# Moving the large tiles by 32 bytes, and four ways to run the products of the last feed-forward

## The chip, the cores and the metric

The kernel runs on one core of a Trainium2 chip. The metric is the device time of one execution in microseconds; the number of a kernel is the median of its runs.

## What is computed

The reference is one inference step of a small hybrid transformer (two layers, model width 2048) for 128 context tokens and 128 latent tokens. The even layer mixes by latent attention and grouped-query attention, the odd one by differential attention. Both end in the same gated feed-forward, the part that the change touches most:

```
def conv_ffn(h, w_up, w_conv, b_conv, w_down):
    u = h @ w_up
    up = jnp.pad(u, ((0, 0), (1, 1), (0, 0)))
    u = up[:, :-2] * w_conv[0] + up[:, 1:-1] * w_conv[1] + up[:, 2:] * w_conv[2] + b_conv
    gate, val = u[..., :D_FF], u[..., D_FF:]
    return (jax.nn.silu(gate) * val) @ w_down
...
    x = x + gt1 * m
    h = rmsnorm(x, g_norm_ffn[l]) * (1 + sc2) + sh2
    x = x + gt2 * conv_ffn(h, w_ffn_up[l], w_ffn_conv[l], b_ffn_conv[l], w_ffn_down[l])
```

All arrays are float32. D_FF is 5632, so w_up has 2048 x 11264 elements and w_down 5632 x 2048.

## The kernel before

Features lie on the 128 partitions and tokens along the row: the 128 context and 128 latent tokens together make 256 columns (NT). Each weight matrix comes in blocks of 128 x 128. One output chunk of 128 features is a product over KD = 16 blocks (up) or KQ = 22 blocks (down).

**Three matmuls per block.** Every float32 operand is split into a high part, rounded to the matmul's type float32r, and a low part, the rest. `split` (lines 243 to 245) does it: ScalarE casts, VectorE subtracts. Weights arrive by DMA in `raw` tiles of 1 MB and are split into `wh` and `wl`, four buffers each of 8 blocks. Activations are kept split, the high 256 columns and the low 256 columns side by side in one row of ROW = 512 elements: `hx` for the input of a stage, one tile `g` per 128 features for the input of the down product. `gemm` (line 330) then issues three matmuls per block into one accumulator bank `acc`: high weights by high columns, high weights by low columns, low weights by high columns. All matmuls pass through line 104, so the profile shows them under that line and they are told apart by their tiles: `acc<-hx,wh` and `acc<-hx,wl` in the up product, `acc<-g,wh` and `acc<-g,wl` in the down product. `acc` has three banks.

**The feed-forward** (`ffn`, line 1226) runs twice, l = 0 and l = 1. The hidden features are done in NQ = 2 halves. For each half, `up` makes 22 pairs of gate and value chunks (44 products of 48 matmuls), and `conv` (line 1236) takes each from its bank by one ScalarE and two VectorE operations; the gated result is split into a `g` tile. Then `down` makes 16 chunks (16 products of 66 matmuls), and `residual` (line 753) adds each to `x` by two VectorE operations, one per token group (L755 in the profile). In the last half of l = 1 ScalarE also squares each finished chunk for the final norm. The first three products of each up stage are made before `ffn` begins, beside the norm, and handed over in `ready`.

**The tail.** After the last chunk's residual come the square (L196), four small matmuls, the root (L208, L211), a diagonal (L231), a spread over the partitions by matmul, and the final scaling (L1348, L1346) with the output DMAs.

**The order.** The instructions of each engine are ordered by a scheduler that simulates the program's timeline, except where `keep_order` pins an instruction to the program's order. DMAs of weights are issued on the SP queue.

**Where tiles lie.** `cst`, the packed constants, is the first tile of the pool `keep`; all other tiles come behind it and start at multiples of 32 bytes. `cst` has 1397 columns, 5588 bytes, and the next tile `x` starts at byte 6752 of each partition. Two unused pads stand in the program: 48 columns ahead of the weight buffers, and SHIFT = 320 bytes ahead of `cv` and `g` (and of `hxc` and `u`). The `g` tiles have one name with 22 rotating buffers.

Of the kernel before, what the change touches and what calls it, by code (L numbers as in the profile page):

```python
# [11 lines left out]
F32R = mybir.dt.float32r  # L12
# [5 lines left out]
P = 128  # L18
# [3 lines left out]
NT = 2 * T  # L22
ROW = 2 * NT
SHIFT = 320
NL = 2
# [6 lines left out]
NQ = 2  # L32
KQ = NFF // NQ
# [6 lines left out]
    ("cond", 32), ("bada", NL * 6 * KD),  # L40
    ("gmix", NL * KD), ("gffn", NL * KD), ("gfin", 16),
    ("gmq", 6), ("gmkv", 4), ("gqn", 1), ("gkn", 1), ("lam", 4),
    ("gsub", 256),
]
_AT = {}
_n = 0
# [42 lines left out]
def step_kernel(ctx: ExitStack, tc: tile.TileContext, A: dict):  # L89
# [4 lines left out]
    def keep_order(i):  # L94
        if not any(i is j for j in kept):
            kept[:] = [i]
            tc.keep_in_program_order(i)
# [16 lines left out]
    pe = TensorE()  # L114
# [5 lines left out]
    pacc = ctx.enter_context(tc.tile_pool(name="pacc", bufs=3, space=PSUM))  # L120
# [5 lines left out]
    def banks(name):  # L126
        return tc.tile_pool(name=name, bufs=1, space=PSUM)
# [3 lines left out]
    def nm(s):  # L131
        uid[0] += 1
        return f"{s}_{uid[0]}"

    def T_(pl, shape, tag, dt=F32, bufs=None):
        kw = {} if bufs is None else {"bufs": bufs}
        return pl.tile(shape, dt, tag=tag, name=nm(tag), **kw)
# [18 lines left out]
    x = T_(keep, [P, KD, NT], "x")  # L156
# [31 lines left out]
    def stat_add(st, src, n, eng=pool):  # L188

        st["n"] += 1  # L190
        if st["n"] == 1:
            st["acc"] = T_(keep, [P, NT], "sqacc")
            act.activation(st["acc"], src, AF.Square)
            return
        sq = T_(tmp, [P, NT], "sq", bufs=2)
        act.activation(sq, src, AF.Square)  # L196
        if st["n"] == n:
            st["last"] = sq
        else:
            eng.tensor_tensor(out=st["acc"], in0=st["acc"], in1=sq, op=ALU.add)  # L200
# [126 lines left out]
            pin(pe.matmul(ps[c][:, :NT], wl, xh(k), start=False, stop=b))  # L327
        return [p[:, :NT] for p in ps]

    def gemm(blocks, xh, xl, n=NT, first=0, between=None):  # L330

        fixed = lambda i: keep_order(i) if between is not None else i
        ps = T_(pacc, [P, 512], "acc")
        last = len(blocks) - 1
        for i in range(last + 1):
            k = (i + first) % (last + 1)
            wh, wl = blocks[k]
            fixed(pe.matmul(ps[:, :n], wh, xh(k), start=(i == 0), stop=False))  # L340
            fixed(pe.matmul(ps[:, :n], wh, xl(k), start=False, stop=False))
            if callable(between):
                if i == (last + 1) // 2:
                    between()
            elif between and i in between:
                between[i]()
            fixed(pe.matmul(ps[:, :n], wl, xh(k), start=False, stop=(i == last)))
        return ps[:, :n]


# [209 lines left out]
    def pump(rows, feats=0.0, until=None):  # L560

        until = until or RLIMIT[stage[0]]
        step()
        side_pump()
        ada["due"] += rows
        while ada["due"] >= 0.25:
            if ada["i"] >= until and not later:
                ada["due"] = 0.0
                break
            ada["due"] -= 0.25 if ada["i"] >= until else 0.25 * ada["pew"]  # L570
            row_step(until)
        feat["due"] += feats
        while feat["due"] >= 1.0 and feat["i"] < FLIMIT[stage[0]]:
            feat["due"] -= 1.0
            feature_step()
# [176 lines left out]
    def residual(ps, l, which, c, st=None):  # L752
        for g in range(2):
            s = slice(g * T, (g + 1) * T)
            dve.scalar_tensor_tensor(out=x[:, c, s], in0=ps[:, s],  # L755
                                     scalar=mod[:, l, 3 * which + 2, c, g:g + 1],
                                     in1=x[:, c, s], op0=ALU.mult, op1=ALU.add)
        if st is not None:
            stat_add(st, x[:, c], KD)
# [465 lines left out]

    def ffn(hx, W, ready, turn, l, st):
        xh, xl = (lambda k: hx[:, k, :NT]), (lambda k: hx[:, k, NT:2 * NT])
        product = lambda: ready.pop(0) if ready else gemm(W.chunk(), xh, xl, between=in_order.pop(0) if in_order else None)
        WD = Weights(A["w_down"][l], KQ, TB)
        cw = ada["cw"]  # L1230
        with tc.tile_pool(name=f"ffn{l}", bufs=1) as fp, banks(f"pffn{l}") as pf:
            feat["home"], feat["pool"] = fp, pf
            feat["due"] = 0.0
            in_order = [{}, {}] + turn + [{}]
            T_(fp, [P, SHIFT // 4], "pad")

            def conv(m):
                early = bool(ready)
                pin = keep_order if early else lambda i: i
                ps = product()  # L1240
                y = T_(fp, [P, NT], "cv", bufs=3)
                pin(act.activation(y, ps, AF.Identity, scale=cw[:, 1, m:m + 1], bias=cw[:, 3, m:m + 1]))  # L1242
                y3 = y.rearrange("p (g t) -> p g t", g=2)
                p3 = ps.rearrange("p (g t) -> p g t", g=2)
                pin(dve.scalar_tensor_tensor(out=y3[:, :, 1:], in0=p3[:, :, :T - 1],  # L1245
                                             scalar=cw[:, 0, m:m + 1], in1=y3[:, :, 1:],
                                             op0=ALU.mult, op1=ALU.add))
                pin(dve.scalar_tensor_tensor(out=y3[:, :, :T - 1], in0=p3[:, :, 1:],  # L1248
                                             scalar=cw[:, 2, m:m + 1], in1=y3[:, :, :T - 1],
                                             op0=ALU.mult, op1=ALU.add))  # L1250
                if early and ready:
                    W.ahead(pin)
                return y

            def up(q):
                gs = []
                for i in range(q * KQ, (q + 1) * KQ):
                    rate = 0 if i < LATE else FRATE["up"]
                    fine[0] = False
                    gate = conv(i)  # L1260
                    pump(0, rate)
                    val = conv(NFF + i)
                    pump(0, rate)
                    act.activation(gate, gate, AF.Silu)
                    dve.tensor_tensor(out=val, in0=gate, in1=val, op=ALU.mult)
                    g = T_(fp, [P, ROW], "g", F32R, bufs=KQ)
                    split(g[:, :NT], g[:, NT:2 * NT], val)
                    gs.append(g)
                    if i == LATE - 1:
                        load_row()  # L1270
                return gs

            def down(gs, q):
                u, rows = None, None
                if q == NQ - 1 and l < NL - 1:
                    u = raw_tile(keep, "hx")
                    rows = raw_rows(u, l + 1, 0)
                for c in range(KD):
                    quiet = q == NQ - 1 and c >= KD - QUIET[0]
                    fine[0] = quiet  # L1280
                    if q == 0:
                        ensure(l, 5, [c // 4])
                    ps = gemm(WD.chunk(), lambda k: gs[k][:, :NT], lambda k: gs[k][:, NT:2 * NT])
                    residual(ps, l, 1, c, st if q == NQ - 1 else None)
                    if rows:
                        rows(c)
                    if l == NL - 1 and q == NQ - 1 and c in EARLY:
                        act.activation(x[:, c], x[:, c], AF.Identity, scale=C("gfin")[:, c:c + 1])
                    pump(0, 0 if quiet else FRATE["down"])
                return u  # L1290

            for q in range(NQ):
                gs = up(q)
                u = down(gs, q)
            while feat["i"] < FLIMIT[stage[0]]:
                feature_step()
            return u


    with banks("pab") as ppool["ada"]:  # L1300
# [3 lines left out]
        first = {1: load_half(1, 0, "araw"), 0: load_half(0, 0, "raw")}  # L1304
        half_unit(1, 0, first[1], keep_order)
        st = stat_init()
# [5 lines left out]
        st = stat_init()  # L1312
        with tc.tile_pool(name="beside", bufs=1) as beside:
            o = mixer_ab(hx, rb0, beside)
            with tc.tile_pool(name="raw", bufs=1) as rp:
# [3 lines left out]
                W = Weights(A["w_up"][0], KD, 1)  # L1319
                hx, *begun = modulated(st, 0, 1, W, u, (keep, "hx"), rp)  # L1320
    stage[0] = "ffn0"
    st = stat_init()
    u = ffn(hx, W, *begun, 0, st)
    stage[0] = "c"
    with tc.tile_pool(name="cc", bufs=1) as cp, banks("pc") as ppool["ada"]:
# [3 lines left out]
        W = Weights(A["w_in_c"], KD, 1)  # L1329
        hx, *begun = modulated(st, 1, 0, W, u, (cp, "hxc"), cp)  # L1330
        load_cw(1)
        st = stat_init()
        ada["pew"] = PEW["c"]
        u = mixer_c(cp, hx, W, begun[0], st)
        W = Weights(A["w_up"][1], KD, 1)
        hx, *begun = modulated(st, 1, 1, W, u, (keep, "hx"), cp)
    stage[0] = "ffn1"
    st = stat_init()
# [52 lines left out]
def _layout(i):  # L1391
    f = {}
# [12 lines left out]
    f["gmq"], f["gmkv"] = _feat(i["g_mla_q"][0]), _feat(i["g_mla_kv"][0])  # L1405
    f["gqn"], f["gkn"] = _feat(i["g_gqa_q"][0]), _feat(i["g_gqa_k"][0])
    f["lam"] = np.stack([i[n][0] for n in ("lambda_q1", "lambda_q2", "lambda_k1", "lambda_k2")], -1)
    f["gsub"] = np.broadcast_to(i["g_diff_sub"][0], (P, 256))
    a = {"cst": np.concatenate([f[n].reshape(P, w) for n, w in _FIELDS], 1)}

    a["wconv"] = _feat(np.concatenate([i["w_ffn_conv"], i["b_ffn_conv"][:, None]], 1))
    xs = np.stack([i["x_prompt"][0], i["x_sample"][0]])
# [71 lines left out]
```

## Time and profile before

| | us |
|---|---|
| median of 2 runs | 2344.56 (2343.95 to 2345.18) |
| span of the profiled execution | 2343.4 |
| TensorE busy / share | 2301.2 / 98% |
| first row of the last feed-forward's down product (half 1, half 2) | 1850.4, 2209.4 |
| last matmul of the last down product starts | 2329.0 |

The span runs from the first to the last instruction of the profiled execution. TensorE busy is the time in which at least one matmul was under way; matmuls overlap each other, so their rate is read from start to start and not from their durations. A slice view of the page shows the same from start to end (40 slices of 58.6 us, busy share in tenths):

```profile
PE   6999999999999999999999999999999999999997
DVE  3569767789999999999988888797899755666654
ACT  4245545575553355555564444456655434555543
PEclk9999999999999999999999999999999999999999
```

TensorE (PE) is full in all slices but the first and the last. VectorE (DVE) is at its fullest in the first feed-forward (slices 9 to 20, about 500 to 1180 us) and has more room in the last one (slices 28 to 39, about 1640 to 2330 us). PEclk, the clock that TensorE was granted, is at 0.9 or more throughout.

### The profile page before, as it was taken

To read this page: it belongs to the slowest core of one execution; us is meant where nothing else is said; L and a number is where in the kernel's file an instruction comes from. 1 tells how busy PE (TensorE), PEld (TensorE's weight loads), DVE (VectorE), ACT (ScalarE), POOL (GpSimd) and SP (SyncE) were. 2 spreads that over 40 slices of the span, in tenths; PEclk is the share of its full clock that TensorE was granted. 3 is DMA by queue.
4 is the path that set the end of the run, shared out by engine and by line. 5 is a ranking of instruction groups with operands and counts; after the bars stand their busy time and mean duration, and the time that the engine had idled before them with its cause. 6 is when DMAs were issued, how large, how long until landed. Compare 5 with 4: busy or idle time off the path is not lost.

```text
span 2343.4 us, 47891 instructions
## 1 busy us (share of the span) xinstructions
PE 2301.2 (98%) x19650; PEld 2182.7 (93%) x19650; DVE 1852.7 (79%) x2879; ACT 1194.5 (51%) x1979; POOL 177.4 (8%) x250
## 2 busy tenths in 40 slices
PE   6999999999999999999999999999999999999997
PEld 4788768999999999999989999999999999999997
DVE  3569767789999999999988888797899755666654
ACT  4245545575553355555564444456655434555543
POOL 0002101210000000001130000023000000000011
PEclk9999999999999999999999999999999999999999
DMA  9988888677767777777778888777677555555553
GB/s 367 358 326 290 305 320 331 231 285 259 262 253 290 293 266 266 270 260 261 284 272 287 308 307 293 259 261 257 243 260 267 196 198 191 189 196 198 194 189 122
DMA packets 106524, 612.98 MB, mean 262 GB/s; under 512 B 11520, under 2 KB 19392, under 8 KB 38592
## 3 DMA queue, kind: packets, MB, share of 16 engines
q1 hardware_dynamic: 106304, 609.92, 71.8%
q8 instruction: 154, 2.52, 0.4%
q14 instruction: 66, 0.54, 0.1%
HBM read 605.12 MB, written 4.75 MB: 260 GB/s over the span
## 4 chain that ended last, share of the span: by engine, by line
PE 94%; DVE 2%; DMA 2%; ACT 1%; issue 1%; POOL 0%; SPq 0%; DVEq 0%; ACTq 0%; POOLq 0%
PE acc L104 86%; PE ada L104 4%; PE att L104 2%; DMA raw<-w_in_ab 1%; PE att L107 1%; DMA araw<-w_ada 1%; DVE wl L245 1%; PE misc L104 1%; PE ada L107 0%; ACT wh L244 0%; POOL block L736 0%; DVE aacc L488 0%; DVE x L1348 0%; DVE nt L603 0%; ACT p L787 0%
## 5 line engine op out<-in xcount | busy, mean ns | idle before, releaser
L244 ACT CAST wh<-raw 128x1024 fp32r<-128x1024 f32 (+2 forms) x824 | 795.2, 976 | 938.6 <-PE acc L104 742.9
L104 PE MATMUL acc<-hx,wh 128*128 128x256 f32 (+1 forms) x7296 | 1260.5, 278 | 5.7 <-ACT hx L613 4.3
L245 DVE TENSOR_TENSOR wl<-raw,wh 128x1024 fp32r<-128x1024 f32 (+2 forms) x824 | 919.1, 1132 | 302.1 <-ACT wh L244 296.9
L104 PEld LDWEIGHTS acc<-hx,wh 128*128 128x128 f32 x7296 | 1102.3, 188 | 39.0 <-issue 19.2
L104 PE MATMUL acc<-hx,wl 128*128 128x256 f32 (+1 forms) x3648 | 1011.4, 278 | 4.5 <-DVE wl L245 4.5
L104 PEld LDWEIGHTS acc<-hx,wl 128*128 128x128 f32 x3648 | 686.4, 188 | 9.8 <-DVE wl L245 5.5
L104 PE MATMUL acc<-g,wh 128*128 128x256 f32 x2816 | 478.9, 276 | 0.0
L104 PEld LDWEIGHTS acc<-g,wh 128*128 128x128 f32 x2816 | 424.0, 188 | 0.0
L104 PE MATMUL acc<-g,wl 128*128 128x256 f32 x1408 | 388.6, 276 | 0.0
L459 DVE CUSTOM_DVE_ANT_0 junk<-araw,condb 128x2048 f32<-128x2048 f32 x120 | 275.9, 2299 | 0.0
L104 PE MATMUL acc<-hxc,wh 128*128 128x256 f32 (+1 forms) x1536 | 267.5, 278 | 1.1 <-DVE hxc L740 1.1
L104 PEld LDWEIGHTS acc<-g,wl 128*128 128x128 f32 x1408 | 264.3, 188 | 0.0
L104 PEld LDWEIGHTS acc<-hxc,wh 128*128 128x128 f32 x1536 | 233.0, 188 | 1.8 <-DVE hxc L740 1.3
L104 PE MATMUL acc<-hxc,wl 128*128 128x256 f32 (+1 forms) x768 | 218.4, 284 | 0.0
L200 POOL TENSOR_TENSOR sqacc<-sqacc,sq 128x256 f32<-128x256 f32 x62 | 68.5, 1105 | 1512.9 <-ACT sq L196 1512.6
L488 DVE SCALAR_TENSOR_TENSOR aacc<-block,condw,aacc 128x512 f32<-128x512 f32 x240 | 170.9, 747 | 7.4 <-DMA block<-w_ada 7.2
L104 PEld LDWEIGHTS acc<-hxc,wl 128*128 128x128 f32 x768 | 144.7, 188 | 15.8 <-issue 11.3
L104 PE MATMUL ada<-araw,condw 128*32 128x512 f32 (+1 forms) x736 | 94.2, 591 | 13.8 <-DMA araw<-w_ada 13.8
L1242 ACT ACTIVATE cv<-acc,convw 128x256 f32<-128x256 f32 x170 | 94.8, 557 | 0.0
L755 DVE SCALAR_TENSOR_TENSOR x<-acc,mod,x 128x128 f32<-128x128 f32 x192 | 57.8, 343 | 41.7 <-PE acc L104 41.6
L1248 DVE SCALAR_TENSOR_TENSOR cv<-acc,convw,cv 128x254 f32<-128x254 f32 x170 | 81.4, 479 | 3.3
L1245 DVE SCALAR_TENSOR_TENSOR cv<-acc,convw,cv 128x254 f32<-128x254 f32 x170 | 80.7, 475 | 0.0
(224 smaller groups left out, 1404.6 us busy)
## 6 DMA issues: line engine op xcount, KB each, us to landing
raw<-w_up SPq DMA_DIRECT2D x176, 1024.0 KB, 4.8
araw<-w_ada SPq DMA_DIRECT2D x146, 1024.0 KB, 5.4
raw<-w_down SPq DMA_DIRECT2D x88, 1024.0 KB, 4.8
raw<-w_in_c SPq DMA_DIRECT2D x48, 1024.0 KB, 6.5
block<-w_ada SPq DMA_DIRECT2D x128, 256.0 KB, 5.3
raw<-w_in_ab SPq DMA_DIRECT2D x19, 1024.0 KB, 7.5
raw<-w_out_ab SPq DMA_DIRECT2D x16, 1024.0 KB, 7.4
raw<-w_out_c SPq DMA_DIRECT2D x16, 1024.0 KB, 6.2
```

What stands on the lines that cost most here:

```text
L104: return self.placed(nc.tensor.matmul(*a, **kw))
L107: return self.placed(nc.tensor.transpose(*a, **kw))
L200: eng.tensor_tensor(out=st["acc"], in0=st["acc"], in1=sq, op=ALU.add)
L244: pin(act.copy(out_hi, src))
L245: pin(dve.tensor_tensor(out=out_lo, in0=src, in1=out_hi.bitcast(F32), op=ALU.subtract))
L459: keep_order(dve.tensor_tensor_reduce(out=T_(feat["pool"], [P, D], "junk"), in1=feat["row"][:, c], in0=feat["raw"].rearrange("p g n -> p ( ...
L488: i = dve.scalar_tensor_tensor(out=acc[c], in0=block, scalar=condw[:, k, c:c + 1], in1=acc[c], op0=ALU.mult, op1=ALU.add)
L755: dve.scalar_tensor_tensor(out=x[:, c, s], in0=ps[:, s], scalar=mod[:, l, 3 * which + 2, c, g:g + 1], in1=x[:, c, s], op0=ALU.mult, op1=AL ...
L1242: pin(act.activation(y, ps, AF.Identity, scale=cw[:, 1, m:m + 1], bias=cw[:, 3, m:m + 1]))
L1245: pin(dve.scalar_tensor_tensor(out=y3[:, :, 1:], in0=p3[:, :, :T - 1], scalar=cw[:, 0, m:m + 1], in1=y3[:, :, 1:], op0=ALU.mult, op1=ALU.add))
L1248: pin(dve.scalar_tensor_tensor(out=y3[:, :, :T - 1], in0=p3[:, :, 1:], scalar=cw[:, 2, m:m + 1], in1=y3[:, :, :T - 1], op0=ALU.mult, op1=A ...
```

## The change

Four edits:

1. **32 bytes.** A field `space` of 8 columns of zeros is added at the end of `cst`. The tile grows by 32 bytes and everything allocated behind it moves by 32 bytes.
2. **Rows.** The `g` tiles get a name each, one buffer per name. In the last feed-forward unused tiles are put ahead of every second of them (64 bytes each; 96 ahead of number 16, 128 ahead of number 20), so that the 22 rows start at eleven different places modulo 512 bytes.
3. **Backwards.** `gemm` can run with the columns of the moving operand and of the accumulator in reversed order; the sums are the same. In the last feed-forward's up stage every second product does, and in its down stage the chunks with c % 4 == 1.
4. **512 columns.** A new `wide_product` makes one matmul of 512 columns of the high weights with the whole row (high and low columns side by side) into a full bank, and one of 256 columns of the low weights with the high columns. The low columns' product then stands in the second half of the bank, and `residual` runs twice, once for each half. The last feed-forward's down stage uses it in the chunks with c % 4 of 2 and 3, backwards in those with 3.

```diff
@@ _FIELDS
-    ("gsub", 256),
+    ("gsub", 256), ("space", 8),
@@ step_kernel
+    def wide_product(blocks, xs, back=False):
+
+        ps = T_(pacc, [P, 512], "acc")
+        flip = (lambda a: a[:, ::-1]) if back else (lambda a: a)
+        last = len(blocks) - 1
+        for k in range(last + 1):
+            wh, wl = blocks[k]
+            pe.matmul(flip(ps), wh, flip(xs(k)), start=(k == 0), stop=False, skip_group_check=True)
+            pe.matmul(flip(ps[:, :NT]), wl, flip(xs(k)[:, :NT]), start=False, stop=(k == last),
+                      skip_group_check=True)
+        return ps[:, :NT], ps[:, NT:]
+
-    def gemm(blocks, xh, xl, n=NT, first=0, between=None):
+    def gemm(blocks, xh, xl, n=NT, first=0, between=None, back=False):
...
+        flip = (lambda a: a[:, ::-1]) if back else (lambda a: a)
...
-            fixed(pe.matmul(ps[:, :n], wh, xh(k), start=(i == 0), stop=False))
-            fixed(pe.matmul(ps[:, :n], wh, xl(k), start=False, stop=False))
+            fixed(pe.matmul(flip(ps[:, :n]), wh, flip(xh(k)), start=(i == 0), stop=False))
+            fixed(pe.matmul(flip(ps[:, :n]), wh, flip(xl(k)), start=False, stop=False))
...
-            fixed(pe.matmul(ps[:, :n], wl, xh(k), start=False, stop=(i == last)))
+            fixed(pe.matmul(flip(ps[:, :n]), wl, flip(xh(k)), start=False, stop=(i == last)))
@@ ffn
-        product = lambda: ready.pop(0) if ready else gemm(W.chunk(), xh, xl, between=in_order.pop(0) if in_order else None)
+        turned = [False]
+
+        def product():
+            if ready:
+                return ready.pop(0)
+            turned[0] = l == NL - 1 and not turned[0]
+            return gemm(W.chunk(), xh, xl, between=in_order.pop(0) if in_order else None, back=turned[0])
...
-                    g = T_(fp, [P, ROW], "g", F32R, bufs=KQ)
+                    j = i % KQ
+                    if l == NL - 1 and q == 0 and j and j % 2 == 0:
+                        T_(fp, [P, {16: 24, 20: 32}.get(j, 16)], f"space{j}x", bufs=1)
+                    g = T_(fp, [P, ROW], f"g{j}x", F32R, bufs=1)
...
-                    ps = gemm(WD.chunk(), lambda k: gs[k][:, :NT], lambda k: gs[k][:, NT:2 * NT])
-                    residual(ps, l, 1, c, st if q == NQ - 1 else None)
+                    if l == NL - 1 and c % 4 > 1:
+                        a, b = wide_product(WD.chunk(), lambda k: gs[k], c % 4 == 3)
+                        residual(b, l, 1, c)
+                        residual(a, l, 1, c, st if q == NQ - 1 else None)
+                    else:
+                        ps = gemm(WD.chunk(), lambda k: gs[k][:, :NT], lambda k: gs[k][:, NT:2 * NT],
+                                  back=l == NL - 1 and c % 4 == 1)
+                        residual(ps, l, 1, c, st if q == NQ - 1 else None)
@@ _layout
+    f["space"] = np.zeros((P, 8), np.float32)
```

## The prediction

> **What bounds the kernel now.** I read the page first, for the busy shares:
>
> ```profile
> span 2343.4 us, 47891 instructions
> ...
> PE 2301.2 (98%) x19650; PEld 2182.7 (93%) x19650; DVE 1852.7 (79%) x2879; ACT 1194.5 (51%) x1979; POOL 177.4 (8%) x250
> ```
>
> TensorE is busy 98% of the span, so a microsecond counts only if it goes off TensorE or off the tail. A busy share says nothing of how fast the matmuls follow each other, so the next view is the chain of waits, first of the last feed-forward and the tail, then of the first feed-forward:
>
> ```profile
> 1622.94 17.93 PE acc L104 x150
> 1640.87 0.44 PE misc L107 x4
> 1641.30 687.97 PE acc L104 x6070
> ...
> 2329.30 0.62 DVE x L755 x2
> ```
>
> ```profile
> 490.96 691.06 PE acc L104 x6096
> ```
>
> The columns are start, microseconds, engine, tile, line and count. From 1641.30 to 2329.3 us the chain is one unbroken row of matmuls: 687.97 / 6070 = 113.3 ns from one to the next, and 691.06 / 6096 = 113.4 ns in the other feed-forward. Nothing is waited for there: what one matmul costs, the kernel pays.
>
> Two views show that 113.3 ns is not a fixed law. The row of 150 before 1641 us has 17.93 / 150 = 119.5 ns; and in the differential attention the timeline of TensorE reads:
>
> ```profile
> 1470.23 0.28 PE L104 MATMUL acc<-hxc,wl 128*128 128x256 f32 x1
> ...
> 1471.29 0.28 PE L104 MATMUL acc<-hxc,wl 128*128 128x256 f32 x1
> ```
>
> Between these two lie nine matmul starts, (1471.29 - 1470.23) / 9 = 117.8 ns. The operation, shape and operands are those of the fast stretches. So the stream has two paces, 113.3 and 117.8 ns. Both last over dozens of matmuls, and the one changes to the other where something else comes between (here the four misc matmuls at 1640.87 us). In the two feed-forwards nothing comes between, and they stay in the fast pace from end to end. I call this the phase of the stream, as a name, not as an explanation.
>
> The window of the last feed-forward shows how much cover the other engines have:
>
> ```profile
> 1641.00:2322.00 681.00, 681.00 (x6011) 681.00 (x6010) 476.20 (x629) 341.31 (x449) 15.46 (x13) 1.00 0.58 207
> ```
>
> In order these are TensorE, its weight loads, VectorE, ScalarE and GpSimd busy, then the granted clock (1.00), the DMA share and GB/s. VectorE has 681 - 476 = 205 us to spare, ScalarE 340, and the waits of this window add that ScalarE's weight splits stand waiting for TensorE to give buffers back:
>
> ```profile
> ACT wh L244 <- PE acc L104: 282.8, 202, 2.0
> ```
>
> **The change, count by count.** In the last feed-forward (l = 1) the up stage has 88 products of 48 matmuls. Three are made ahead; of the other 85 every second one, beginning with the first, is read and written backwards: 43 x 48 = 2,064 matmuls. The down stage has 32 chunks of 66 matmuls, 2,112 in all. A quarter stays, a quarter (8 x 66 = 528) runs backwards, a quarter is wide, and a quarter wide and backwards. Each of the 16 wide chunks replaces, per block, two 256-column matmuls by one of 512: 352 matmuls and weight loads fewer, 352 wide ones, and 5,632 narrow ones left of 6,336.
>
> *512 columns.* Two narrow ones take 2 x 113.3 = 226.7 ns. No matmul of this kind in the trace has 512 columns; the nearest has 384 (the key and value up-projection), in this row of the chain:
>
> ```profile
> 221.16 4.89 PE acc L104 x28
> ```
>
> That is 4.89 / 28 = 174.6 ns. A line through 256 columns at 113.3 and 384 at 174.6 gives 236 ns for 512; through the slow 117.8 and 174.6 it gives 231. From below, the fp32 matmuls of the attention, which stream longer per column, come off the engine like this in the timeline:
>
> ```profile
> 1243.07 1.46 PE L104 MATMUL att<-dv,pT 128*128 128x256 f32 x6
> ```
>
> ```profile
> L104 PE MATMUL att<-dv,pT x48: 377/379/380, 1243.1 to 1518.0; 128*128 128x256 f32 x48
> ```
>
> Six starts with 0.379 us for the last: (1.46 - 0.379) / 5 = 216 ns. So the 352 blocks bring between 352 x (216 - 226.7) = -3.8 us and 352 x (236 - 226.7) = +3.3 us. I take 231, the nearest in kind with the slow pace at both ends: 352 x 4.3 = +1.5 us. The Trainium skill, "TensorE: Matmul & The Clock Gate", section "Back-to-back issue gap", has a warm matmul cost its columns / 2.4 plus 2.5 ns, that is 216 ns for 512 and by that a gain of 3.8 us. For the 384 columns it says 162.5 ns and the row above says 174.6, so the row decides.
>
> *The second residual.* A wide chunk is added to x in two halves, so 16 chunks bring two more VectorE operations each:
>
> ```profile
> L755 DVE SCALAR_TENSOR_TENSOR x<-acc,mod,x x64: 339/343/352, 1858.5 to 2329.6; 128x128 f32<-128x128 f32 x64
> ```
>
> 32 x 0.343 = 11 us on VectorE, in 205 us of slack, and the accumulator bank is held 0.7 us longer, with three banks and 7.5 us of matmuls per chunk. Hidden, except once: the last chunk (c = 15) is a wide one, and its residual is on the chain at 2329.30 us. There the pair costs its 0.62 us twice: +0.6 us. If the slack weren't there, the cost would be the 11 us.
>
> *Backwards.* No instruction in the trace has a step of -1. From below: if the pace came down to the fastest weight-load-bound one in the trace,
>
> ```profile
> 264.93 0.83 PE L104 MATMUL att<-pT,vm 128*128 128x128 f32 x6
> ```
>
> ```profile
> L104 PE MATMUL att<-pT,vm x48: 270/275/377, 264.9 to 367.0; 128*128 128x128 f32 x48
> ```
>
> (0.83 - 0.275) / 5 = 111 ns, the 2,064 + 528 narrow ones would bring 2,592 x 2.3 = -6 us. From above: if a reversed row went at the 216 ns of the other attention row, they cost 2,592 x 102.7 = +266 us. I take neither: a reversed row touches the same neighbours in the same number, so I let it cost nothing by itself.
>
> *Rows at eleven places, and 32 bytes.* By the program's allocation the weight buffers start at byte 104,096 of a partition (and every 4,096 on), hx at 28,256, the g rows at 152,160 and every 2,048 on: remainder 32 by 64 each, and every moving row stands 448 bytes past its weights, modulo 512. The new field behind the constants moves all of them together to remainder 0, so the 448 stays everywhere but in the 20 of 22 g rows of the last down stage that lie behind a space; these stand at 10 other distances. Every fast and every slow row above has one and the same distance and remainder, so the trace can't price either edit; the two paces bound what I give them, 0 to +4.5 ns per matmul, and 111 ns from below. The separate names of the g tiles replace 22 rotating buffers one for one and add no wait.
>
> *What I charge.* The last feed-forward, one stream at one pace now, becomes a sequence of stretches of other direction, width and distance. Each boundary is a chance to fall into the slow phase. Between no matmul and all of the 5,632 narrow ones, 0 to 5,632 x 4.5 = 25 us, I choose a quarter: +6.3 us. That quarter is a choice, from nothing better than that stretches of both paces stand side by side where the stream is interrupted.
>
> Sum: 2343.4 + 1.5 + 0.6 + 6.3 = 2351.8 us of span. The median of before, 2344.56, stands 1.2 above the span, so 2353 us. Without the slow phase it is 2347, with all of it 2372.
>
> **Rivals.** *Backwards is slow (slower side).* A reversed run of fp32 into the accumulator, or out of the row, loses whatever joins neighbours, and goes at half pace. Then +266 us for the narrow ones, and the 8 wide backward chunks have 176 wide (+216 at most) and 176 narrow matmuls (+103): 56 us. Time 2345 + 322 = 2667 us. For it: no reversed access stands anywhere in the trace. Against: a reversed row holds the same addresses, one beside the other. It decides from 47 / 2,592 = 18 ns per reversed matmul. The Trainium skill, "PSUM — Partial Sum Buffer", section "Specifications (TRN2)", has lines of 8 bytes and says that a non-contiguous pattern slows matmuls significantly; read strictly this covers a step of -1, and no row here can show it. Chance 0.12.
>
> *The 32 bytes help (faster side).* What of the 113.3 ns the 256 columns themselves cost isn't separated in the trace. If a part is paid because every row begins off a multiple of 64 bytes, all matmuls gain, down to the 111 ns of the row: some 17,500 of this kind (12,166 in the two chain rows, the rest in the mixers) x 2.3 = -40 us, 2304 us; half of it 2325. It passes 2% only if the pace falls below 110.7 ns, under the floor of the row. Against: the slow and the fast pace have the same remainder, so something else sets them. Chance 0.12.
>
> *The 32 bytes hurt.* The whole kernel falls into the slow phase: 17,500 x 4.5 = +79 us, 2424 us. From 60% of the matmuls on it is over 2%. Chance 0.06.
>
> *Nothing happens.* The pace is set by the weight loads, which go forward and keep their width; direction, place and distance are indifferent. Then -3.8 to +3.3 for the blocks and +0.6: 2341 to 2348 us, near 2345. Chance 0.20.
>
> **How the numbers follow.** The forecast has the remaining 0.50, at 2353 us, with 2347 to 2372 as its own range. 2% of 2344.6 is 47 us, about what a measurement of this kernel can tell from no change: below 2298 counts as faster, above 2391 as slower. Faster: 0.03, the far end of the help by 32 bytes. Slower: 0.12 for the backward rows, 0.05 of the hurt, and 0.01 for the forecast's tail, 0.18. The rest, 0.79, is within. The range from 2312 to 2385 takes in forecast, nothing and most of the help; left out are the slow reversed reads (0.12), the hurt (0.06) and the far end of the help (0.02).
>
> **What would show it.** In the chain of waits after the change the first feed-forward's row tells the 32 bytes alone: 113.4 ns again if they do nothing, 111 or 118 if a rival is right. In the last feed-forward the timeline tells the rest: the spacing of backward against forward products in the up stage (equal by my forecast but for stretches at 118), the spacing of the wide matmuls (231 ns, or 216, or 236), and within a forward narrow down chunk the spacing by row (if it steps with the eleven places, the distance counts and my phase is only a name). The tail should be 0.6 us longer. I am wrong if a spacing above 135 ns appears in the backward products, or if the first feed-forward changes its pace.

## The result and the profile after

| | before | after |
|---|---|---|
| median of 2 runs, us | 2344.56 (2343.95 to 2345.18) | 2367.18 (2367.14 to 2367.21) |
| span of the profiled execution, us | 2343.4 | 2365.4 |
| row of matmuls of the last feed-forward, us | 687.97 (6070) | 706.38 (5718) |

The kernel is 1.0095 times as long as before [1.0066, 1.0124], 22.6 us more, within the 2% that count as the same. The page of the changed kernel opens with:

```profile
span 2365.4 us, 47211 instructions
...
PE 2322.1 (98%) x19298; PEld 2187.7 (92%) x19298; DVE 1860.4 (79%) x2911; ACT 1192.5 (50%) x1979; POOL 176.1 (7%) x250
```

There are 352 matmuls fewer, and TensorE is busy 20.9 us longer. The chain of waits (start, us, engine, tile, line, count) says where, at the same places as before:

```profile
493.75 691.06 PE acc L104 x6096
...
1626.64 17.83 PE acc L104 x150
1644.47 0.44 PE misc L107 x4
1644.91 706.38 PE acc L104 x5718
...
2351.31 1.14 DVE x L768 x4
```

The first feed-forward has its 691.06 us to the hundredth. The last one has 18.4 us more with 352 matmuls fewer. The last residual has 1.14 us for 0.62. From it to the end lie 14.1 us in both kernels, since the 0.52 us are made good by a pair of matmuls of the tail, which takes 0.69 us here and 1.21 before; over the runs below that pair takes between 0.68 and 1.21, whatever the edit. The other 3.6 us of the span came before 1644.91 us, in code that the change leaves alone but for the place of its tiles: the first row begins 2.8 us later. In the runs below, it begins anywhere from 490.1 to 494.6 us, and kernels that are the same up to there differ as much. So 18.4 us are the change, and most of the remaining 3.6 cannot be told from the variation between executions.

The timeline of TensorE gives the 18.4 us piece by piece. Its columns are start, us, engine, line, operation, tiles, shapes and count. The first four lines bound three up products of 48 matmuls, the next five four down chunks, and the rest lie within a plain down chunk:

```profile
1652.80 0.40 PE L104 MATMUL acc<-hx,wh 128*128 128x256 f32 x2
...
1658.45 0.40 PE L104 MATMUL acc<-hx,wh 128*128 128x256 f32 x2
...
1663.91 0.40 PE L104 MATMUL acc<-hx,wh 128*128 128x256 f32 x2
...
1669.56 0.40 PE L104 MATMUL acc<-hx,wh 128*128 128x256 f32 x2
...
1873.92 0.40 PE L104 MATMUL acc<-g0x,wh 128*128 128x512 f32 x1
...
1881.66 0.40 PE L104 MATMUL acc<-g0x,wh 128*128 128x512 f32 x1
...
1889.43 0.40 PE L104 MATMUL acc<-g0x,wh 128*128 128x256 f32 x2
...
1889.78 0.39 PE L104 MATMUL acc<-g1x,wh 128*128 128x256 f32 x2
...
1890.12 0.39 PE L104 MATMUL acc<-g2x,wh 128*128 128x256 f32 x2
...
1890.47 0.40 PE L104 MATMUL acc<-g3x,wh 128*128 128x256 f32 x2
...
1890.83 0.40 PE L104 MATMUL acc<-g4x,wh 128*128 128x256 f32 x2
...
1892.59 0.39 PE L104 MATMUL acc<-g9x,wh 128*128 128x256 f32 x2
...
1892.93 0.39 PE L104 MATMUL acc<-g10x,wh 128*128 128x256 f32 x2
...
1897.16 0.40 PE L104 MATMUL acc<-g0x,wh 128*128 128x256 f32 x2
...
1904.97 0.40 PE L104 MATMUL acc<-g0x,wh 128*128 128x512 f32 x1
```

The two backward up products take 5.65 us each (117.7 ns a matmul), the forward one between them 5.46 (113.8, where 113.3 would be 5.44). All 41 backward products that lie whole in this row of the chain are so, and the 41 forward ones between them come back to 113.3 ns, after three to five matmuls of 114 to 124. From 1873.92 on, the starts of g0x bound four down chunks: wide 7.74 us, wide and backwards 7.77, plain 7.73, backwards 7.81. Before, 66 matmuls at 113.3 ns made 7.48. Of the 4,080 up matmuls 3,958 lie in the row of 706.38 us. The 122 ahead of it (two and a half products) are no part of the 18.4 us; in the kernel before they were slow already, the first two of these products with 117.8 ns a matmul. So the account of that row, with means over all chunks of a kind worked out from the starts in the trace:

| part | count x extra | us |
|---|---|---|
| backward up products | (41 x 48 + 22) x 4.42 ns | 8.8 |
| first matmuls of the forward up products | 41 x 48 x 0.3 ns | 0.6 |
| plain down chunks (rows moved) | 8 x 0.25 us | 2.0 |
| backward down chunks | 8 x 0.33 us | 2.6 |
| wide | 8 x 0.26 us | 2.1 |
| wide and backwards | 8 x 0.29 us | 2.3 |

That makes 18.4 us, as the chain has it. No part gains anything, the wide chunks with 44 matmuls in place of 66 included.

Within the plain chunk from 1889.43 us the spacing steps with the row. Rows 1 and 9 take 0.34 us for their three matmuls, row 3 takes 0.36. Rows 1 and 9 stand 448 and 192 bytes past their weights modulo 512, so what they share is the 192 modulo 256. (Rows 0 and 8 share it too, but each comes right behind slow matmuls.) In this way the rows raised the question that the experiments are about. From here on, *distance* is the byte address of a moving row less that of its weights, modulo 256, by the program's allocation. In the kernel before it is 192 for every 256-column row of `g`, `hx` and `hxc`, against `wh` and `wl` alike.

### The profile page after: what moved, and what is told of

The parts are those of the page before. It is cut to its first block, busy times and chain, and to the rows that moved or that the text cites. A ratio compares the mean times of both kernels' runs of the same rounds, so it can differ in the third digit from the quotient of the medians.

```text
span 2365.4 us, 47211 instructions
## 1 busy us (share of the span) xinstructions
PE 2322.1 (98%) x19298; PEld 2187.7 (92%) x19298; DVE 1860.4 (79%) x2911; ACT 1192.5 (50%) x1979; POOL 176.1 (7%) x250
## 4 chain that ended last, share of the span: by engine, by line
PE 94%; DVE 3%; DMA 1%; ACT 1%; issue 1%; POOL 0%; SPq 0%; DVEq 0%; ACTq 0%; POOLq 0%
PE acc L104 86%; PE ada L104 4%; PE att L104 2%; PE att L107 1%; DVE wl L245 1%; DMA raw<-w_in_ab 1%; PE misc L104 1%; DMA araw<-w_ada 0%; ACT wh L244 0%; PE ada L107 0%; POOL block L749 0%; DMA x<-xT 0%; DVE aacc L501 0%; DVE x L1377 0%; DVE proj L957 0%
## 5 line engine op out<-in xcount | busy, mean ns | idle before, releaser
L104 PE MATMUL ada<-araw,condw 128*32 128x512 f32 (+1 forms) x736 | 94.6, 594 | 15.2 <-ACT sq L196 13.5
L768 DVE SCALAR_TENSOR_TENSOR x<-acc,mod,x 128x128 f32<-128x128 f32 x224 | 66.9, 343 | 43.5 <-PE acc L104 43.3
L104 PEld LDWEIGHTS ada<-araw,condw 128*32 128x32 f32 x736 | 16.5, 111 | 32.0 <-ACT sq L196 13.4
L957 DVE TENSOR_TENSOR proj<-proj,acc 128x256 f32<-128x256 f32 x44 | 17.9, 417 | 30.5 <-PE acc L104 30.5
L196 ACT ACTIVATE sq<-x 128x256 f32<-128x256 f32 x75 | 30.6, 411 | 15.6 <-DVE x L768 13.7
L1285 DVE TENSOR_TENSOR cv<-cv,cv 128x256 f32<-128x256 f32 x88 | 37.1, 422 | 1.3
```

Source lines behind the costliest of these rows:

```text
L104: return self.placed(nc.tensor.matmul(*a, **kw))
L768: dve.scalar_tensor_tensor(out=x[:, c, s], in0=ps[:, s], scalar=mod[:, l, 3 * which + 2, c, g:g + 1], in1=x[:, c, s], op0=ALU.mult, op1=AL ...
```

## The experiments

Each is an edit of the kernel before, and is compared with it on the same chip (medians of before there: 2346.46 us for the first four, 2344.98 for the next four, 2346.34 for the last four). In each fence stand the rows of the first and the last feed-forward in the chain of waits; undisturbed they have 691.06 and 687.97 us.

### The parts of the change, one by one

**32 bytes alone.**

```diff
-    ("gsub", 256),
+    ("gsub", 256), ("space", 8),
```

> Only the field of 32 bytes is added. Theory A (absolute places mean nothing to the matmuls): both feed-forwards keep 113.3 ns, and the median stays within 1 us of before; the 2.8 us that the changed kernel's first feed-forward began late were chance. Rival B (the 32 bytes cost time in the mixers ahead of it): the first feed-forward starts 2 to 4 us later again and the median is 2 to 4 us above before.

2347.31 us, ratio 1.0008 [1.0000, 1.0017]. The chain:

```profile
493.40 691.06 PE acc L104 x6096
...
1644.08 687.97 PE acc L104 x6070
```

Both rows are those of before to the hundredth: 12,166 matmuls don't notice that all tiles moved together. The first row begins 2.4 us later than in the profile before, as the rival said, but the medians are 0.85 us apart, and kernels that are the same up to there begin it as far apart. An effect ahead of the first feed-forward, of 0 to 4 us by the interval, stays open.

**Rows alone.**

```diff
-                    g = T_(fp, [P, ROW], "g", F32R, bufs=KQ)
+                    j = i % KQ
+                    if l == NL - 1 and q == 0 and j and j % 2 == 0:
+                        T_(fp, [P, {16: 24, 20: 32}.get(j, 16)], f"space{j}x", bufs=1)
+                    g = T_(fp, [P, ROW], f"g{j}x", F32R, bufs=1)
```

> Only the rows at eleven places, last feed-forward, all products forward and narrow. Theory A (the distance of a moving row to its weights sets the pace): each of the 32 down chunks goes from 7.48 to 7.73 us as the plain chunks of the changed kernel do, +8.0 us in all, the up stage stays at 113.3 ns. Rival B (the plain chunks were slow only because a slow stretch went before them): the down stage stays at 113.3 ns, +0 us.

2353.29 us, 1.0029 [1.0017, 1.0041]. The chain:

```profile
1642.48 696.31 PE acc L104 x6070
```

8.34 us more, over 2,112 down matmuls 3.95 ns each: the down stage runs at 117.28 ns, the up stages at 113.3. An edit that changes no matmul, only addresses, costs 8 us in this row (the medians are 6.8 us apart). That is theory A's forecast; the rival falls.

**The up stage backwards, all of it.**

```diff
+    def gemm(blocks, xh, xl, n=NT, first=0, between=None, back=False):
...
+        flip = (lambda a: a[:, ::-1]) if back else (lambda a: a)
...
+        product = lambda: ready.pop(0) if ready else gemm(W.chunk(), xh, xl, between=in_order.pop(0) if in_order else None, back=l == NL - 1)
```

> All 85 products of the last up stage run backwards, nothing else is changed, so the direction never turns within the stage. Theory A (a reversed row meets its weights in another way, at every matmul): 117.75 ns throughout, 85 x 48 x 4.42 ns = +18 us. Rival B (turning from one direction to the other throws the stream out of the fast pace): only one turn per half, 113.3 ns after it, +0 to 1 us.

2368.69 us, 1.0096 [1.0082, 1.0110]. The chain, and then the window view of its two down stages, which run forwards as before (bounds, length, TensorE busy and its matmuls, weight loads, VectorE, ScalarE, granted clock, DMA share, GB/s; a count takes in two or three matmuls cut by the bounds):

```profile
1640.74 710.25 PE acc L104 x6070
```

```profile
1858.00:1982.00 124.00, 124.00 (x1055) 124.00 (x1054) 10.07 (x32) 0.56 (x1) 1.00 0.53 186
...
2231.20:2350.00 118.80, 118.80 (x1050) 118.80 (x1049) 10.06 (x32) 0.56 (x1) 1.00 0.46 163
```

22.3 us more. The backward products run at 117.8 ns, and 3,958 of their matmuls lie in this row: 3,958 x 4.45 = 17.6 us, as theory A has it. The rest comes from the first down stage, which neither theory foresaw: it is unchanged, and stays at 117.8 ns from end to end (1,056 x 4.45 = 4.7 us), while the second one, behind the same kind of products, is back at 113.3 after four matmuls. At the distance of 192 both paces can hold for 1,000 matmuls.

**The wide chunks alone**, forwards, rows unmoved.

```diff
+                    if l == NL - 1 and c % 4 > 1:
+                        a, b = wide_product(WD.chunk(), lambda k: gs[k])
+                        residual(b, l, 1, c)
+                        residual(a, l, 1, c, st if q == NQ - 1 else None)
```

> Only the 16 wide chunks, forward, rows where they were. Theory A (a wide matmul costs 232 ns by itself and the narrow one behind it 119): 352 x (351.8 - 340.0) = +4.2 us and 0.6 us of the second residual, +4.8 us. Rival B (the wide ones were slow because of the places of the rows): 226.7 + 113.3 ns per block, +0.6 us. Rival C (columns / 2.4 plus 2.5 ns): 216 + 113.3, -3.8 + 0.6 = -3.2 us.

2363.68 us, 1.0074 [1.0060, 1.0088], far more than the 352 wide blocks themselves account for. The chain, then starts of chunks in the timeline (a wide one, two narrow ones, the next wide one), then the window of the second up stage:

```profile
1640.93 706.15 PE acc L104 x5718
```

```profile
1872.73 0.40 PE L104 MATMUL acc<-g,wh 128*128 128x512 f32 x1
...
1880.51 0.40 PE L104 MATMUL acc<-g,wh 128*128 128x256 f32 x2
...
1888.28 0.40 PE L104 MATMUL acc<-g,wh 128*128 128x256 f32 x2
...
1896.05 0.40 PE L104 MATMUL acc<-g,wh 128*128 128x512 f32 x1
```

```profile
1973.80:2222.30 248.50, 248.50 (x2113) 248.50 (x2112) 42.24 (x90) 24.04 (x43) 1.00 0.53 186
```

A wide chunk takes 7.78 us: per block 235 ns for the wide matmul and 118.3 for the narrow one behind it, 353.3 in place of 340. That is 16 x 22 x 13.3 ns = 4.7 us, near theory A's 4.2 for them; rivals B and C fall. The other 13.5 us are paid by matmuls that the edit doesn't touch, and no theory had them. From the first wide chunk on, the 14 narrow down chunks that follow one take 7.77 us instead of 7.48 (4.1 us), and the whole second up stage, 2,112 matmuls of hx, runs at 117.8 ns (9.4 us). 4.7 + 4.1 + 9.4 = 18.2, and the chain has 706.15 - 687.97 = 18.2. Alone, the wide chunks cost the feed-forward what all four edits cost together (18.4): the parts do not add up, because a part sets the pace of what follows it.

### The distance

If the distance sets the pace of a forward stream, each of its eight multiples of 32 has a pace of its own. The pad ahead of g grows by one amount in the first feed-forward and by another in the last, so that each kernel measures two. The weights and `hx` stay; the tiles of the feed-forward behind the pad, `cv` among them, move along.

```diff
-            T_(fp, [P, SHIFT // 4], "pad")
+            T_(fp, [P, (SHIFT + (256, 64)[l]) // 4], "pad")
```

> All g rows of the first feed-forward 256 bytes further on, all of the last one 64 bytes, nothing else. Theory A (the distance to the weights counts, modulo 256): the first down stage stays at 113.3 ns, the last one goes to 117 to 118 ns throughout, 2112 x 4.2 ns = +9 us. Rival B (modulo 512): both go to 117 to 118 ns, +18 us. Rival C (only unlike distances one after the other are slow): both stay at 113.3 ns, +0 us.

2360.95 us, 1.0073 [1.0050, 1.0095].

```profile
492.19 691.06 PE acc L104 x6096
...
1642.97 702.03 PE acc L104 x6070
```

256 bytes change nothing, 64 bytes cost 14.06 us, or 6.66 ns for each of 2,112: 120.0 ns. Only theory A has one stage slow and one not, though it had 117 to 118 ns for the slow one. The next three differ in the two numbers of the pad alone, (128, 192), (32, 96) and (160, 224):

> The g rows 128 bytes further on in the first feed-forward, 192 in the last. Theory A (distance modulo 256): both are other than before and both down stages go at 117 to 118 ns, +18 us. Rival C (only unlike distances are slow): +0 us.

2367.73 us, 1.0094 [1.0064, 1.0123].

```profile
494.57 700.46 PE acc L104 x6096
...
1654.65 699.25 PE acc L104 x6070
```

> The g rows 32 bytes further on in the first feed-forward, 96 in the last. Theory A: neither is the distance of before, both between 113.3 and 118 ns; if the distance can also gain, one of these steps of 32 bytes is where 111 ns would show. Rival C: +0 us.

2362.73 us, 1.0074 [1.0051, 1.0097].

```profile
491.26 701.66 PE acc L104 x6096
...
1652.37 695.03 PE acc L104 x6070
```

> The g rows 160 bytes further on in the first feed-forward, 224 in the last. Theory A: as for 32 and 96, between 113.3 and 118 ns in each; the eight distances of these four kernels together give the pace by distance. Rival C: +0 us.

2368.36 us, 1.0096 [1.0067, 1.0126].

```profile
491.31 705.14 PE acc L104 x6096
...
1656.93 696.42 PE acc L104 x6070
```

Each row's excess over 691.06 or 687.97, divided by 2,112, gives the extra of that distance; the steady spacings in the traces, alike in the two halves of a feed-forward, agree:

| moved by | distance | ns a matmul |
|---|---|---|
| 0, 256 | 192 | 113.3 |
| 32 | 224 | 118.3 |
| 64 | 0 | 120.0 |
| 96 | 32 | 116.7 |
| 128 | 64 | 117.8 |
| 160 | 96 | 120.0 |
| 192 | 128 | 118.7 |
| 224 | 160 | 117.3 |

One distance of eight is fast, and the kernel before has it everywhere. The up stages stayed at 113.3 ns in all four kernels, also behind a slow down stage. The 22 rows of the run with the rows alone, each taken at its distance in this table, would have a mean of 117.4 ns; the run had 117.28. (Single rows there differ more, by what goes ahead of them.)

That it is the distance to the weights is argued by leaving out: 32 bytes on the rows alone cost 5 ns a matmul, 32 bytes on rows and weights together cost nothing, so it is neither the row's own place nor its place against the accumulator, which did not move. No run moves the weights alone, and a distance to tiles that other engines use is not ruled out.

### Is there a distance at which backwards is fast?

One theory: a reversed row has a good distance too, only another one, and slow stretches are left again at the good distance. The rival: a reversed row is slow wherever it stands. Both down stages are run wholly backwards, the rows moved by 64 in the first feed-forward and 128 in the last, then by 192 and 32.

```diff
-            T_(fp, [P, SHIFT // 4], "pad")
+            T_(fp, [P, (SHIFT + (64, 128)[l]) // 4], "pad")
...
-                    ps = gemm(WD.chunk(), lambda k: gs[k][:, :NT], lambda k: gs[k][:, NT:2 * NT])
+                    ps = gemm(WD.chunk(), lambda k: gs[k][:, :NT], lambda k: gs[k][:, NT:2 * NT], back=True)
```

> Both down stages wholly backwards, g rows 64 bytes further on in the first feed-forward and 128 in the last; the up stages as before. Theory A (backwards is slow because a reversed row needs another distance than a forward one): one of the four distances of this run and the next gives 113.3 ns backwards. Rival B (a reversed row is slower at every distance): 117 to 120 ns in both, +18 to 28 us. Forward the two distances gave 120.0 and 117.8 ns.

2387.78 us, 1.0179 [1.0159, 1.0200]. The chain, and the window of the second up stage of the first feed-forward, which runs forwards and is unchanged:

```profile
490.59 711.02 PE acc L104 x6096
...
1660.89 711.41 PE acc L104 x6070
```

```profile
824.80:1073.10 248.30, 248.30 (x2110) 248.30 (x2110) 41.62 (x88) 24.00 (x43) 1.00 0.70 255
```

Backwards at +64 goes at 118.3 ns, at +128 at 120.0 (10.6 and 14.1 us). The other 9.4 us of each row are the second up stage, which stays at 117.8 ns, as in the kernel with the wide chunks.

> As the run before, with 192 and 32 bytes. Forward these gave 118.7 and 118.3 ns. Theory A: 113.3 ns at one of the four. Rival B: 117 to 120 ns, +18 to 28 us.

2370.15 us, 1.0104 [1.0084, 1.0124].

```profile
494.15 705.18 PE acc L104 x6096
...
1658.73 697.37 PE acc L104 x6070
```

14.12 and 9.40 us: 120.0 ns at +192, 117.8 at +32, and here the up stages are back at 113.3. With the unmoved rows (117.8 in the up products) five of the eight distances are measured, and none is fast backwards. That speaks for the rival; +96, +160 and +224 weren't tried. Yet backwards isn't slower than forwards everywhere: at +32 and +64 it has 117.8 and 118.3 ns where forwards has 118.3 and 120.0, at +128 and +192 it has 120.0 for 117.8 and 118.7. What a reversed row loses for certain is the fast pace at the distance of before. Row and accumulator were only reversed together, so which of the two costs it is open.

### What ends a slow stretch

In the changed kernel forward up products recover behind backward ones, while behind wide chunks the stage stays slow. If both paces are stable at distance 192, and what goes ahead decides which holds, one backward product at the head of the second up stage should free that stage in the kernel with the wide chunks.

```diff
+                if l == NL - 1 and q == 1:
+                    turned.append(True)
...
+        product = lambda: ready.pop(0) if ready else gemm(W.chunk(), xh, xl, between=in_order.pop(0) if in_order else None, back=turned.pop() if turned else False)
```

> The kernel with the wide chunks alone, in which the second up stage ran at 117.8 ns from end to end, with the first product of that stage backwards. Theory A (at the distance of before both paces are stable, and what goes ahead decides which one it is): the reversed product lets the stream out, products 2 to 44 at 113.3 ns, 9.2 us less than with the wide chunks alone, about +8 us over before. Rival B (the wide chunks slow the up stage behind them for another reason): 117.8 ns stays, about +17 us.

2356.27 us, 1.0045 [1.0030, 1.0060]; with the wide chunks alone it was 2363.68. The chain, and the starts of the first three products of that stage in the timeline:

```profile
1644.87 696.39 PE acc L104 x5718
```

```profile
1977.72 0.40 PE L104 MATMUL acc<-hx,wh 128*128 128x256 f32 x2
...
1983.37 0.41 PE L104 MATMUL acc<-hx,wh 128*128 128x256 f32 x2
...
1988.83 0.39 PE L104 MATMUL acc<-hx,wh 128*128 128x256 f32 x2
```

5.65 us for the backward product, 5.46 for the next one (spacings of 118, 125 and 118 ns, then 113), and 113.3 ns for the rest of the stage. The row is 706.15 - 696.39 = 9.8 us shorter. 43 products of 48 matmuls and the two narrow chunks behind them are back at 113.3 ns, (2,064 + 132) x 4.45 = 9.8 us. The same matmuls, at the same addresses, ran at 117.8 ns without the one reversed product ahead of them. That is theory A's forecast. (The medians, taken on two chips, are 7.4 us apart; in the profiled executions the row begins 3.9 us later here, ahead of the edit.)

**Can it be used on the kernel before?** Its differential attention has slow stretches of its own at distance 192 (the 117.8 ns at 1470 us in the prediction). Two of the 16 blocks of each input product there are run backwards.

```diff
+    def gemm(blocks, xh, xl, n=NT, first=0, between=None, turns=()):
...
+            flip = (lambda a: a[:, ::-1]) if i in turns else (lambda a: a)
...
-            return ready.pop(0) if ready else gemm(W.chunk(), xh, xl, between=middle)
+            return ready.pop(0) if ready else gemm(W.chunk(), xh, xl, between=middle, turns=(0, 9))
```

> Before, with two of the 16 blocks of each input product of the differential attention backwards (the first, and the second one behind the interruption in the middle), where the stream is found in both paces. If three reversed matmuls let it out of the slow pace: up to some 500 slow matmuls fewer, -2 us. If they throw it into the slow pace as often as out: 0. If mostly in: up to 1,500 more, +7 us.

2347.13 us, 1.0001 [0.9992, 1.0011]: no gain. Counted in threes from start to start, with those between 115.5 and 122 ns called slow, some 750 of 2,180 of these matmuls are slow, against some 560 in the profile before. Short turns slow more matmuls than they free. No version here beats the kernel before.

## Why the prediction was right, and where it was not

The time, 2367, lies in the range and 14 us above the point. The sum foretold 7.8 us more in the last feed-forward; it was 18.4. That the range held is in part luck: above the point it was drawn for slow stretches that come by chance, and what filled it were matmuls that are slow for another reason.

**What held.** TensorE alone sets the time, and the other engines hide the second residuals: VectorE has 7.7 us more work in all, and only the last pair shows, 0.52 us for the 0.6 charged. The 32 bytes do nothing to the matmuls of the feed-forwards, by the row of the first one and by a run of their own; both rivals about them fall. The bound "with all of it 2372" was nearly reached, by other matmuls than it counts: some six in ten of the narrow ones were in slow stretches, some by more than the 4.5 ns, and the wide ones paid too. The size of the price was about right, the number of matmuls that pay it wasn't. Backwards at half pace falls as well: it needed 18 ns per reversed matmul to pass 2%, and the runs show 4.4 to 6.7 over the fast pace; the wide ones lose 2.2, with 234.6 ns backwards against 232.4 forwards in the changed kernel. The Trainium skill, "PSUM — Partial Sum Buffer", section "Specifications (TRN2)", says that a non-contiguous pattern slows matmuls significantly. Here a step of -1 in row and accumulator costs 4% at the distance of before, and nothing against forward rows at +32 and +64.

**The step that failed: the charge for the slow phase, "I choose a quarter: +6.3 us".** The prediction made the slow pace a matter of chance at boundaries. In the changed kernel it isn't one. Every reversed product and nearly every moved row is slow, by its direction and its distance, and the plain up products, which have the most boundaries, lose 0.6 us in all. The charge should have been the count of reversed matmuls and moved rows. With the 4.45 ns that the prediction had in sight, 2,592 narrow reversed ones make 11.5 us, and the 528 narrow ones of the plain chunks up to 2.3; the wide chunks, which this leaves out, measured 4.4.

**Two steps ahead of it failed with it.** "a reversed row touches the same neighbours in the same number, so I let it cost nothing by itself": it costs 4.4 ns at the distance of before, and is the largest term, 8.8 of 18.4 us. "the trace can't price either edit": true of the rows, and they got no charge of their own; alone they cost 8.3 us. Their bound of 4.5 ns, from the slow pace in sight, was also too low, since two distances cost 6.7.

**512 columns.** 231 ns were taken; the runs have 232.4 in the changed kernel and 235 alone, near the upper bound of 236. The 216 ns of the Trainium skill, "TensorE: Matmul & The Clock Gate", section "Back-to-back issue gap", which the section gives as the gap of an isolated matmul, are not reached in this stream in either run. What was not priced is the narrow matmul behind each, at 118 to 119 ns, so a block costs 12 to 13 ns more than before and not 4.3.

**The rival "Nothing happens"** had direction, place and distance indifferent. The rows alone (8.3 us) and the backward up stage (22.3 us) refute it. Nor is 2% "about what a measurement of this kernel can tell from no change": the intervals above reach 0.3% to either side at most.

**The phase.** "if it steps with the eleven places, the distance counts and my phase is only a name": it does, and the distance counts. Yet the name stands for something at distance 192, where 113.3 and 117.8 ns are both stable, and what ran before can decide which one holds. In the changed kernel this spared time: as in the run with one backward product ahead of the second up stage, its reversed products free the forward ones between them, where the wide chunks alone leave all 2,112 slow.

**Open.** Why the distance modulo 256 matters, why a reversed row isn't fast at any distance tried, and what decides the way out of the slow pace: two equal down stages behind backward products went different ways, and the up stage recovered behind reversed rows at +192 and +32 but not at +64 and +128. No run here looks inside TensorE.

## What to carry to other kernels

When TensorE's stream is the bound, measure its spacing from start to start per stage, and keep the placement of moving operands to weights that gives the fastest one: an edit that moves the one and not the other, such as a new tile between them, can cost 1%. Price an edit to such a stream by the count of matmuls whose direction, width or place it changes, and look for the change in the stages behind it too. Fewer, wider matmuls brought nothing here, where the two narrow ones already follow each other without a gap.

## What the runs showed of the hardware

- The spacing of 256-column float32r matmuls, each with its own weights, depends on where the moving row stands; by the runs above what counts is its distance to the weights modulo 256 bytes: 113.3 ns at 192, 116.7 to 120.0 at the seven other multiples of 32. The Trainium skill, "TensorE: Matmul & The Clock Gate", section "Step-by-step: what each phase is for", has the moving operand and the weights read through two independent ports. By that alone one would not expect this dependence, so the measurement decides; what causes it no run shows.
- At the fast distance there are two stable paces, 113.3 and 117.8 ns, with the granted clock at 1.00 in both, and 2,112 equal matmuls can stay in the slow one without a break.
- Reversed moving rows with reversed accumulators go at 117.8 to 120.0 ns at the five distances measured.
- 512 columns take 232 to 235 ns, more than two times 113.3 (226.7).
